# Split buffers for rounded and low weight halves, a longer lead, and another order of the products in each weight tile

## The chip, the cores and the metric

The kernel runs on one core of a Trainium2 chip. The core has a matrix engine (TensorE, PE in the profile; PEld is its loading of the operand that stays in the array), a vector engine (VectorE, DVE), a scalar engine (ScalarE, ACT), GpSimd (POOL) and SyncE (SP), which here only starts DMA transfers. Each engine works through its own queue of instructions in order; semaphores tie the queues together. The metric is the time of one execution in microseconds (us).

## What is computed

Two residual layers over 256 tokens of width 2048: a stick-breaking attention layer, then a layer whose attention chooses 64 keys for each query with an indexer. Each is followed by a multi-layer perceptron (MLP) with squared ReLU and 8192 hidden features. Cut to what matters here:

```python
for i in range(2):
    h = rms_norm(x, norm_mix[i])
    x = x + (stick_breaking_mixer if i % 2 == 0 else dsa_mixer)(h, ...)
    h = rms_norm(x, norm_mlp[i])
    x = x + jnp.square(jax.nn.relu(h @ w_up[i])) @ w_down[i]
```

All inputs are float32. The weights are about 390 MB and each is read once, so there is one pass over them.

## The kernel before

**Products in two halves.** TensorE multiplies in a rounded float32 format. To keep accuracy, each operand is split: `wh` is the weight tile rounded (ACT copies it into the rounded type, L946 through the helper at L101), `wl` is what the rounding left (DVE subtracts, L947). The activations are kept in the same two halves. Each product is then three matmuls: x high with `wh`, x high with `wl`, x low with `wh` (L217 to L219, and L376 to L378). Where the weights are the stationary operand (`feats_out`), the first and third are one matmul of 512 columns, since both halves of x stand side by side, and `wl` takes one of 256 (L239, L240).

**Tiles.** All weights are cut into tiles of 128 x 1024 (512 KB). The whole program is one list of items. An item has the raw tiles that it loads (`raws`), a `source` that gives the tile to split, a function `mm` that issues its matmuls, and a list `post` of functions to call after them. The main loop (from L968) takes the items in order: for item i it first splits item i + LEAD (LEAD = 2, L979), issues loads as buffers come free (L980), issues the item's matmuls (L981) and then what is in `post`. `wh` and `wl` lie in one tile `w` with three buffers. Raw tiles come in over SP's queue into `wraw` (five buffers) or `sraw` (four).

The order written is not quite the order on the engines: the program is built with a scheduler that draws up each engine's queue with the help of a timeline of its own (L1007). Only the first 16 items, where `pinned` holds, and the instructions marked one by one keep the order as written. Once drawn up, a queue is fixed.

**The MLP in blocks.** The up projection of a block of 1024 features is a product of 2 x 2 blocks, and for seven of the eight blocks in each MLP it is done with seven block products instead of eight (`seven`, L361). This needs sums of weight blocks, made on DVE: for each of four steps s, b11 + b12 (L402), then b12 + b22 on top of that (L403), then t = (b11 + b12) + b22 (L404), all three in `sums`, which is the source of the second of the four items in `first`; later t + b21 (L408), the source of the third of three items in `second`. `first` has 16 items, `second` 12, of six matmuls each. The four `first` items of a step use: b11 itself, b22 (after the sums), the first sum, the second sum.

Between these items stand tiles of the down projection of the block before (`down`, 12 matmuls an item): nine among `first`, then two, then five among `second` (SPAN, L49). So a period has 28 + 16 items. Block products gather in PSUM, in a pair of banks (`pair`) and in single banks `v`, `z`, `y`. `between` and `between2` (L430, L435) combine those after `first`; `after` and `after2` (L439, L445) after `second`, on DVE into `se`. Then ACT applies ReLU and square (`square_up`, L338). `turn` (L449) transposes the finished block on PE (L455), eight transposes into an accumulator, and ACT and DVE split it into the halves of the next down projection's operand (L457 through L101, and L458). `ends` (L460) lists these steps by their distance in items from the end of `second`: 0, 1, 2, 3, 5 and 7 items on, among the items of the next block. The down projection's results are added to the residual on DVE (`add_residual`, L261).

There are three accumulators of two banks each (`accp`): a pair of block products, the running down projection, and the turns share them. Two single banks (`auxp`) serve the rest.

Of the kernel before, what the change touches and what calls it, by code (L numbers as in the profile page):

```python
# [16 lines left out]
P = 128  # L17
D = 2048
S = 256
# [24 lines left out]
RAW = 5  # L44
LEAD = 2
PINNED = 16
# [3 lines left out]
EARLY = 5  # L50
RAWS = {"wraw": RAW, "sraw": 4}
BANK = 128
# [10 lines left out]
class Item:  # L63


    def __init__(self, raws, a, b, mm, moving=False, source=None):
        self.raws, self.a, self.b, self.mm, self.moving, self.post = raws, a, b, mm, moving, []
        self.source = source or (lambda: raws[0].ap)

# [6 lines left out]
def trunk(ctx, tc, x, norm_mix, w_in_a, w_out_a, w_in_b, w_out_b, q_norm_b, k_norm_b, rel_bias,  # L76
# [126 lines left out]
    def tokens_out(items, key, w, r0, c0, lhs, q, done, n=KT, apart=False):  # L203


        def mm(wh, wl):
            if q == 0 and apart:
                accs[key] = [auxp.tile([P, 512], F32, name="aux") for _ in range(2)]
            elif q == 0:
                acc = accp.tile([P, 2, 512], F32, name="acc")  # L210
                accs[key] = [acc[:, t, :] for t in range(2)]
            acc = accs[key]
            for t in range(2):
                for j in range(KB):
                    k = KB * q + j
                    ts = slice(t * P, (t + 1) * P)
                    pin(pe.matmul(acc[t], lhs(k, 0, ts), wh[:, j, :], start=(k == 0), stop=False))  # L217
                    pin(pe.matmul(acc[t], lhs(k, 0, ts), wl[:, j, :], start=False, stop=False))  # L218
                    pin(pe.matmul(acc[t], lhs(k, 1, ts), wh[:, j, :], start=False,  # L219
                                  stop=(k == n - 1)))  # L220
# [8 lines left out]
    def feats_out(items, key, w, c0, q, done):  # L229

        def mm(wh, wl):
            if q == 0:
                accs[key] = accp.tile([P, 2, 512], F32, name="acc")
            acc = accs[key]
            for j in range(KA):
                k = KA * q + j
                for m in range(2):
                    ms = slice(m * P, (m + 1) * P)
                    pe.matmul(acc[:, m, :], wh[:, j, ms], xT[:, k, :, :], start=(k == 0), stop=False)  # L239
                    pe.matmul(acc[:, m, 0:S], wl[:, j, ms], xT[:, k, 0, :], start=False,  # L240
                              stop=(k == KT - 1))
        it = plain(rows(w, KA * P * q, KA * P, c0, 256), KA, 256, mm)
# [3 lines left out]

    def joined(acc):

        c = tmp.tile([P, 2, S], F32, name="jc")
        u = tmp.tile([P, 2, S], F32, name="ju")  # L250
        copy(c, acc[:, :, S:])
        dve.tensor_add(u, acc[:, :, :S], c)
        return u
# [24 lines left out]
    def mlp(l, next_col):  # L278
# [63 lines left out]
        def up_done(h, s, acc):  # L342
            u = joined(acc)
            square_up(u)
# [16 lines left out]
        def seven(f, c0):  # L361
# [8 lines left out]
            def item(raws, bank, x, s, source, opens=True):  # L370
                def mm(wh, wl):
                    acc = bank()
                    on = dict(skip_group_check=not opens)
                    for j in range(KB):
                        k = KB * s + j
                        pe.matmul(acc, x(k, 0), wh[:, j, :], start=opens and k == 0, stop=False, **on)  # L376
                        pe.matmul(acc, x(k, 0), wl[:, j, :], start=False, stop=False, **on)  # L377
                        pe.matmul(acc, x(k, 1), wh[:, j, :], start=False, stop=k == HK - 1, **on)  # L378
                return Item(raws, KB, 512, mm, True, source)

# [15 lines left out]
            for s in range(HK // KB):  # L396
                b11, b12 = block(0, 0, s, "wraw"), block(0, 1, s, "sraw")
                b21, b22 = block(1, 0, s, "sraw"), block(1, 1, s, "sraw")

                def sums(s=s, b11=b11, b12=b12, b22=b22):  # L400
                    t = g["t", s] = temp().rearrange("p (a b) -> p a b", a=KB)
                    dve.tensor_add(b11.ap, b11.ap, b12.ap)  # L402
                    dve.tensor_add(b12.ap, b12.ap, b22.ap)  # L403
                    dve.tensor_add(t, b11.ap, b22.ap)  # L404
                    return b22.ap

                def last_sum(s=s, b21=b21):
# [41 lines left out]
            def turn(n, c0, c1):  # L449
# [3 lines left out]
                for k in range(4):  # L453
# [58 lines left out]
        for f in range(1, LASTF + 1):  # L512
            first, second, mid, ends = seven(f, 1024 * f)
            items += spread(first, ds[:n1])
            for n, e in late:
                items[n].post.append(e)
            at = len(items) - 1
            items += ds[n1:n1 + n2] + spread(second, ds[n1 + n2:n1 + n2 + n3])
            put(items, at, mid)
            at = len(items) - 1  # L520
            late = [(at + n, e) for n, e in enumerate(ends) if e]
            if f == LASTF:
                late = [(at + max(n - 1, 0), e) for n, e in enumerate(e for e in ends if e)]
            ds = ds[n1 + n2 + n3:]
        items += ds
        for n, e in late:
            items[n].post.append(e)
        return items, begin


    def mixer_a():
# [17 lines left out]
        def qk_done(which, hp, acc):  # L549
            u = joined(acc)  # L550
            r = mk([P, 2, S], which + "T")
# [113 lines left out]
    def mixer_b():  # L665
# [42 lines left out]
        def ki_done():  # L708
            acc = accs.pop("ki")
            c = tmp.tile([P, 2, S], F32, name="jc")[:, 0, :]  # L710
            u = tmp.tile([P, 2, S], F32, name="ju")[:, 0, :]
            copy(c[:80, :], acc[:80, 0, S:])
# [224 lines left out]

    def split(i):
        if i < len(items):
            it = items[i]  # L940
            pair = wpool.tile([P, 2 * WT + BANK], F32R, name="w")
            at = SHIFT if it.moving else 0
            wh, wl = (pair[:, at + h * WT:at + h * WT + it.a * it.b].rearrange(
                "p (a b) -> p a b", a=it.a) for h in range(2))
            raw = it.source()
            copy(wh, raw)  # L946
            pin(dve.tensor_sub(wl, raw, wh.bitcast(F32)))  # L947
            parts[i] = wh, wl

    for n in range(4):  # L950
# [60 lines left out]
```

## Time and profile before

| What | Value |
|---|---|
| median of 3 runs | 2174.95 us (2173.22 to 2175.07) |
| the profiled execution's own time | 2174.56 us |
| its span, first to last instruction | 2172.8 us |
| mean granted clock of TensorE | 0.991 |
| read from memory | 391.82 MB, 183 GB/s over the span |
| a 512 KB weight load, issue to landing | 3.5 to 4.6 us (median by tensor) |

The span of one profiled execution is a little shorter than its time, because the time has the start and the end of the execution as well. A row of the timeline reads: start, duration, engine, line, operation, output and input tile, shapes, count; in brackets the engine's idle time before it and what ended it. A row of the list of waits reads: who, for whom, then total us, times, and longest us. Matmuls overlap in the records: a matmul of 512 columns is shown with 0.39 us, though the next begins 0.23 us later, so lengths are taken from start to start. L101 is a helper's line: many of ACT's copies carry it, and the tile's name tells them apart.

### The profile page before, as it was taken

The page shows a single profiled execution, that of the slowest core. Times are in us where ns is not written, and L with a number is a line of the kernel's source. Part 1 is how long each engine was busy: PE and PEld are TensorE (multiplying, and loading weights), DVE is VectorE, ACT ScalarE, POOL GpSimd, SP SyncE. Part 2 cuts the span into 40 slices and gives each one's busy share as a digit, 9 for nine tenths or more (in the row PEclk, how much of TensorE's full clock was granted, in tenths as well). Part 3 has the DMA queues.
Part 4 walks back from the last instruction along what each step waited for, and adds up shares of the span by engine and source line. Part 5 has one row for each costly group of instructions (what it writes and reads, how often), then busy time and mean ns, then how long its engine had stood idle before and what let it go on. Part 6 is the DMA issues. An engine that isn't in the chain of part 4 may idle for free.

```text
span 2172.8 us, 26216 instructions
## 1 busy us (share of the span) xinstructions
PE 2107.2 (97%) x9764; PEld 1720.2 (79%) x9764; DVE 1719.7 (79%) x1833; ACT 1256.8 (58%) x1560; POOL 28.2 (1%) x71
## 2 busy tenths in 40 slices
PE   8999999999999999999999999999999999999999
PEld 7888888877777777777888788887777777777787
DVE  5466665898898888988865877689989898888985
ACT  5455555666566565655654556566656556565563
POOL 0100010000000000000000000000000000000000
PEclk9999999999999999999999999999999999999999
DMA  7667655665555646555466564466555555555544
GB/s 235 191 190 192 177 169 179 200 222 165 191 186 165 222 140 210 176 182 198 140 205 185 158 189 160 151 218 207 171 194 175 186 192 174 196 172 184 180 155 160
DMA packets 241396, 398.85 MB, mean 184 GB/s; under 512 B 14578, under 2 KB 80756, under 8 KB 241268
## 3 DMA queue, kind: packets, MB, share of 16 engines
q1 hardware_dynamic: 233508, 389.74, 55.8%
q10 hardware_dynamic: 7760, 7.43, 1.2%
q8 instruction: 76, 1.25, 0.3%
q14 instruction: 52, 0.43, 0.1%
HBM read 391.82 MB, written 5.23 MB: 183 GB/s over the span
## 4 chain that ended last, share of the span: by engine, by line
PE 70%; DVE 20%; issue 5%; ACT 3%; DMA 2%; DVEq 0%; ACTq 0%
PE acc L218 14%; PE acc L219 14%; PE acc L217 13%; DVE w L947 9%; PE acc L239 7%; PE acc L240 4%; PE acc L377 3%; PE acc L376 3%; PE acc L378 3%; DVE wraw L402 2%; DVE t L404 2%; ACT w L101 2%; DVE sraw L403 2%; DVE xs L261 2%; PE aux L377 2%
## 5 line engine op out<-in xcount | busy, mean ns | idle before, releaser
L947 DVE TENSOR_TENSOR w<-wraw,w 128x1024 fp32r<-128x1024 f32 x626 | 758.1, 1222 | 317.3 <-ACT w L101 312.8
L101 ACT ACTIVATE w<-wraw 128x1024 fp32r<-128x1024 f32 x626 | 664.6, 1062 | 587.3 <-PE acc L219 443.1
L218 PE MATMUL acc<-w,hS 128*128 128x512 f32 x1008 | 402.4, 399 | 10.0 <-DVE w L947 9.1
L217 PE MATMUL acc<-w,hS 128*128 128x512 f32 x1008 | 398.5, 396 | 0.1
L219 PE MATMUL acc<-w,hS 128*128 128x512 f32 x1008 | 398.0, 395 | 0.0
L239 PE MATMUL acc<-xT,w 128*128 128x512 f32 x896 | 314.2, 391 | 0.0
L101 ACT ACTIVATE w<-sraw 128x1024 fp32r<-128x1024 f32 x224 | 237.9, 1062 | 112.8 <-PE acc L219 60.8
L947 DVE TENSOR_TENSOR w<-sraw,w 128x1024 fp32r<-128x1024 f32 x224 | 273.4, 1221 | 27.8 <-ACT w L101 23.7
L240 PE MATMUL acc<-xT,w 128*128 128x256 f32 x896 | 253.4, 284 | 1.4 <-DVE w L947 1.2
L218 PEld LDWEIGHTS acc<-w,hS 128*128 128x128 f32 x1008 | 193.3, 192 | 59.4 <-DVE w L947 21.3
L217 PEld LDWEIGHTS acc<-w,hS 128*128 128x128 f32 x1008 | 192.1, 191 | 44.7 <-ACT w L101 4.0
L219 PEld LDWEIGHTS acc<-w,hS 128*128 128x128 f32 x1008 | 192.6, 191 | 39.8
L239 PEld LDWEIGHTS acc<-xT,w 128*128 128x128 f32 x896 | 168.1, 188 | 33.8
L240 PEld LDWEIGHTS acc<-xT,w 128*128 128x128 f32 x896 | 169.3, 189 | 3.9 <-DVE w L947 2.6
L217 PE MATMUL acc<-w,xT 128*128 128x512 f32 x320 | 127.8, 399 | 2.5 <-ACT w L101 2.5
L218 PE MATMUL acc<-w,xT 128*128 128x512 f32 x320 | 126.5, 395 | 0.5 <-DVE w L947 0.5
L219 PE MATMUL acc<-w,xT 128*128 128x512 f32 x320 | 126.4, 395 | 0.0
L376 PE MATMUL acc<-w,xS 128*128 128x512 f32 x224 | 94.8, 423 | 9.1 <-ACT w L101 9.1
L218 PE MATMUL acc<-w,oT 128*128 128x512 f32 x256 | 101.7, 397 | 0.0
L217 PE MATMUL acc<-w,oT 128*128 128x512 f32 x256 | 101.0, 395 | 0.0
L219 PE MATMUL acc<-w,oT 128*128 128x512 f32 x256 | 100.3, 392 | 0.0
L261 DVE SCALAR_TENSOR_TENSOR xs<-acc,rs,xs 128x512 f32<-128x512 f32 x120 | 84.3, 744 | 18.0 <-PE acc L219 18.0
(207 smaller groups left out, 3033.4 us busy)
## 6 DMA issues: line engine op xcount, KB each, us to landing
wraw<-in_w_down_dram SPq DMA_DIRECT2D x256, 512.0 KB, 4.6
sraw<-in_w_up_dram SPq DMA_DIRECT2D x168, 512.0 KB, 4.5
wraw<-in_w_in_a_dram SPq DMA_DIRECT2D x96, 512.0 KB, 4.0
wraw<-in_w_up_dram SPq DMA_DIRECT2D x88, 512.0 KB, 4.5
wraw<-in_w_in_b_dram SPq DMA_DIRECT2D x64, 512.0 KB, 3.7
wraw<-in_w_out_a_dram SPq DMA_DIRECT2D x32, 512.0 KB, 3.5
wraw<-in_w_out_b_dram SPq DMA_DIRECT2D x32, 512.0 KB, 3.8
bv_d<-bv ACTq DMA_DIRECT2D x4, 766.0 KB, 8.8
```

The source lines that it names most:

```text
L101: pin(act.activation(o, i, AF.Copy, scale=scale))
L217: pin(pe.matmul(acc[t], lhs(k, 0, ts), wh[:, j, :], start=(k == 0), stop=False))
L218: pin(pe.matmul(acc[t], lhs(k, 0, ts), wl[:, j, :], start=False, stop=False))
L219: pin(pe.matmul(acc[t], lhs(k, 1, ts), wh[:, j, :], start=False, stop=(k == n - 1)))
L239: pe.matmul(acc[:, m, :], wh[:, j, ms], xT[:, k, :, :], start=(k == 0), stop=False)
L240: pe.matmul(acc[:, m, 0:S], wl[:, j, ms], xT[:, k, 0, :], start=False, stop=(k == KT - 1))
L261: dve.scalar_tensor_tensor(xc, acc[t], scale[:, t:t + 1], xc, op0=OP.mult, op1=OP.add)
L376: pe.matmul(acc, x(k, 0), wh[:, j, :], start=opens and k == 0, stop=False, **on)
L377: pe.matmul(acc, x(k, 0), wl[:, j, :], start=False, stop=False, **on)
L378: pe.matmul(acc, x(k, 1), wh[:, j, :], start=False, stop=k == HK - 1, **on)
L402: dve.tensor_add(b11.ap, b11.ap, b12.ap)
L947: pin(dve.tensor_sub(wl, raw, wh.bitcast(F32)))
```

## The change

1. `wh` and `wl` get tiles of their own, with LEAD + 2 = 5 and LEAD + 1 = 4 buffers; LEAD is 3. In the main loop the low half of item i + 3 is made, then loads are issued, then the rounded half of item i + 4.
2. Each item's matmuls with `wh` come first, those with `wl` after them.
3. The three sums are no longer one step. The second item of a step has b22 itself as its source, the third item's source makes the first sum, the fourth's the second; the third sum comes after the fourth item's low half (`then`). `b11`, `b12` and `b22` are held until there. `sraw` has five buffers.
4. `ends` are placed by the us of the items' matmuls (2.72 an item, half of it for block items) instead of by their number: 0, 1.4, 1.4, 2.8, 8.0 and 10.8 us. The second step of the sums after `second` thereby comes one item later, the second turn one item earlier; in the last block, where whole items follow, the second step moves one item later.
5. Room: the tile `ju` of `joined` moves from a pool shared by all sections into the sections (in the MLP it takes a `t2` buffer), and the scratch for dynamic DMA is cut to 1024. `between2` is attached to the same item as before.
6. At the start three items are split before the first matmul, with the rounded half of a fourth, and the second half of the first 512 columns of x is transposed before the first item's matmuls instead of behind them.

```diff
-LEAD = 2
+LEAD = 3
+TURNS = (8.0, 10.8)
-RAWS = {"wraw": RAW, "sraw": 4}
+RAWS = {"wraw": RAW, "sraw": 5}
...
-            for t in range(2):
-                for j in range(KB):
-                    k = KB * q + j
-                    ts = slice(t * P, (t + 1) * P)
-                    pin(pe.matmul(acc[t], lhs(k, 0, ts), wh[:, j, :], start=(k == 0), stop=False))
-                    pin(pe.matmul(acc[t], lhs(k, 0, ts), wl[:, j, :], start=False, stop=False))
-                    pin(pe.matmul(acc[t], lhs(k, 1, ts), wh[:, j, :], start=False,
-                                  stop=(k == n - 1)))
+            for w, parts in ((wh, (0, 1)), (wl, (0,))):
+                for t in range(2):
+                    for j in range(KB):
+                        k = KB * q + j
+                        for part in parts:
+                            pin(pe.matmul(acc[t], lhs(k, part, slice(t * P, (t + 1) * P)), w[:, j, :],
+                                          start=w is wh and part == 0 and k == 0,
+                                          stop=w is wl and k == n - 1))
...
-                def sums(s=s, b11=b11, b12=b12, b22=b22):
-                    t = g["t", s] = temp().rearrange("p (a b) -> p a b", a=KB)
-                    dve.tensor_add(b11.ap, b11.ap, b12.ap)
-                    dve.tensor_add(b12.ap, b12.ap, b22.ap)
-                    dve.tensor_add(t, b11.ap, b22.ap)
-                    return b22.ap
+                def two(b11=b11, b12=b12):
+                    dve.tensor_add(b11.ap, b11.ap, b12.ap)
+                    return b11.ap
+
+                def other(b12=b12, b22=b22):
+                    dve.tensor_add(b12.ap, b12.ap, b22.ap)
+                    return b12.ap
+
+                def three(s=s, b11=b11, b22=b22):
+                    t = g["t", s] = temp().rearrange("p (a b) -> p a b", a=KB)
+                    dve.tensor_add(t, b11.ap, b22.ap)
...
                 first += [item([b11], pair(0), quarter(0, 0), s, lambda b=b11: b.ap),
-                          item([b12, b22], single("v"), summed(3), s, sums),
-                          item([], single("z"), summed(0), s, lambda b=b11: b.ap),
-                          item([], pair(1), summed(2), s, lambda b=b12: b.ap)]
-                first[-2].uses = [b11]
-                first[-1].uses = [b12]
+                          item([b22], single("v"), summed(3), s, lambda b=b22: b.ap),
+                          item([b12], single("z"), summed(0), s, two),
+                          item([], pair(1), summed(2), s, other)]
+                first[-1].then, first[-1].uses = three, [b11, b12, b22]
...
-            ends = [after, after2,
-                    lambda: (square_up(se(2)), square_up(se(1))),
-                    lambda: (square_up(se(0)), square_up(g["s2"])),
-                    None, lambda: turn(1, se(2), se(1)), None, lambda: turn(0, se(0), g["s2"])]
+            ends = [(0, after), (1.4, after2), (1.4, lambda: (square_up(se(2)), square_up(se(1)))),
+                    (2.8, lambda: (square_up(se(0)), square_up(g["s2"]))),
+                    (TURNS[0], lambda: turn(1, se(2), se(1))), (TURNS[1], lambda: turn(0, se(0), g["s2"]))]
...
-    def split(i):
+    def half(it, name, bufs):
+        home = wpool.tile([P, WT + BANK], F32R, name=name, bufs=bufs)
+        at = SHIFT if it.moving else 0
+        return home[:, at:at + it.a * it.b].rearrange("p (a b) -> p a b", a=it.a)
+
+    def high(i):
         if i < len(items):
             it = items[i]
-            pair = wpool.tile([P, 2 * WT + BANK], F32R, name="w")
-            at = SHIFT if it.moving else 0
-            wh, wl = (pair[:, at + h * WT:at + h * WT + it.a * it.b].rearrange(
-                "p (a b) -> p a b", a=it.a) for h in range(2))
-            raw = it.source()
+            wh, raw = half(it, "wh", LEAD + 2), it.source()
             copy(wh, raw)
+            parts[i] = wh, raw
+
+    def low(i):
+        if i < len(items):
+            it = items[i]
+            wh, raw = parts[i]
+            wl = half(it, "wl", LEAD + 1)
             pin(dve.tensor_sub(wl, raw, wh.bitcast(F32)))
             parts[i] = wh, wl
+            if it.then:
+                it.then()
...
-        split(i)
+        high(i)
+        low(i)
         loads(i, 1)
-    items[0].post.append(lambda: prep(0, 0, False, (1,)))
+        if i == 1:
+            prep(0, 0, False, (1,))
+    high(LEAD)
...
-        split(i + LEAD)
+        low(i + LEAD)
         loads(i + LEAD)
+        high(i + LEAD + 1)
         it.mm(*parts.pop(i))
```

More of the change, by code (lines that the diff above doesn't have):

```diff
@@ L67, in __init__ @@
         self.raws, self.a, self.b, self.mm, self.moving, self.post = raws, a, b, mm, moving, []
-        self.source = source or (lambda: raws[0].ap)
+        self.source, self.then, self.us = source or (lambda: raws[0].ap), None, 2.72
 def plain(src, a, b, mm, moving=False):
@@ L234, in mm @@
             acc = accs[key]
[L235 to L241, printed above, removed]
+            for w, cs, xs_ in ((wh, slice(0, 2 * S), slice(0, 2)), (wl, slice(0, S), 0)):
+                for j in range(KA):
+                    k = KA * q + j
+                    for m in range(2):
+                        pe.matmul(acc[:, m, cs], w[:, j, m * P:(m + 1) * P], xT[:, k, xs_, :],
+                                  start=w is wh and k == 0, stop=w is wl and k == KT - 1)
         it = plain(rows(w, KA * P * q, KA * P, c0, 256), KA, 256, mm)
@@ L245, in feats_out, with joined @@
         items.append(it)
-    def joined(acc):
+    def joined(acc, u):
         c = tmp.tile([P, 2, S], F32, name="jc")
-        u = tmp.tile([P, 2, S], F32, name="ju")
         copy(c, acc[:, :, S:])
@@ L342, in up_done @@
         def up_done(h, s, acc):
-            u = joined(acc)
+            u = joined(acc, temp()[:, :2 * S].rearrange("p (a b) -> p a b", a=2))
             square_up(u)
@@ L373, in mm @@
                     on = dict(skip_group_check=not opens)
[L374 to L379, printed above, removed]
+                    for w, parts in ((wh, (0, 1)), (wl, (0,))):
+                        for j in range(KB):
+                            k = KB * s + j
+                            for part in parts:
+                                pe.matmul(acc, x(k, part), w[:, j, :],
+                                          start=opens and w is wh and part == 0 and k == 0,
+                                          stop=w is wl and k == HK - 1, **on)
+                it = Item(raws, KB, 512, mm, True, source)
+                it.us /= 2
+                return it
             def pair(n):
@@ L514, in mlp @@
             items += spread(first, ds[:n1])
[L515 to L523, printed above, removed]
+            put(items, len(items) - 1, mid[:1])
+            items += ds[n1:n1 + n2]
+            put(items, len(items) - n2, mid[1:])
+            items += spread(second, ds[n1 + n2:n1 + n2 + n3])
+            late.append((len(items) - 1, ends))
             ds = ds[n1 + n2 + n3:]
         items += ds
-        for n, e in late:
-            items[n].post.append(e)
+        for n, ends in late:
+            at = 0
+            for us, f in ends:
+                while at < us:
+                    n, at = n + 1, at + items[n + 1].us
+                items[n].post.append(f)
         return items, begin
@@ L549, in qk_done @@
         def qk_done(which, hp, acc):
-            u = joined(acc)
+            u = joined(acc, mk([P, 2, S], "ju"))
             r = mk([P, 2, S], which + "T")
@@ L710, in ki_done @@
             c = tmp.tile([P, 2, S], F32, name="jc")[:, 0, :]
-            u = tmp.tile([P, 2, S], F32, name="ju")[:, 0, :]
+            u = mk([P, S], "ju")
             copy(c[:80, :], acc[:80, 0, S:])
@@ L995 @@
     from concourse.bass_utils import run_bass_kernel_spmd
-    nc = bacc.Bacc("TRN2", target_bir_lowering=False, num_devices=1)
+    nc = bacc.Bacc("TRN2", target_bir_lowering=False, num_devices=1,
+                   dynamic_dma_scratch_size=1024)
     arrays, args = {}, []
```

## The prediction

> **What bounds the kernel now.** I read the busy shares first, then what the TensorE waits for, then each stretch of the multi-layer perceptron (MLP) by itself.
>
> ```profile
> PE 2107.2 (97%) x9764; PEld 1720.2 (79%) x9764; DVE 1719.7 (79%) x1833; ACT 1256.8 (58%) x1560; POOL 28.2 (1%) x71
> ```
>
> The TensorE (PE) is busy 97% of the span. So a change that adds and removes no matmul can only win two things: PE's gaps, and matmuls that run slower than they could. The shares also average stages with different limits. The windows by stage show where the loss lies. Columns: window, its length, then busy time and (instructions) of PE, PEld, DVE, ACT and POOL, then granted clock, DMA share, GB/s.
>
> ```profile
> core 0 of [0], span 2172.8 us
> core 0: us, PE busy (x) PEld busy (x) DVE busy (x) ACT busy (x) POOL busy (x), PEclk, DMA share, GB/s
> 425.00:521.00 96.00, 92.50 (x422) 74.52 (x420) 87.63 (x86) 62.05 (x70) 0.00 (x0) 1.00 0.56 183
> 521.41:981.71 460.30, 439.56 (x1881) 349.38 (x1881) 405.94 (x381) 272.70 (x286) 0.00 (x0) 0.98 0.56 183
> 705.45:797.38 91.93, 87.79 (x377) 69.90 (x377) 81.19 (x77) 54.54 (x58) 0.00 (x0) 0.98 0.57 183
> 1425.00:1564.00 139.00, 135.31 (x655) 111.47 (x653) 124.35 (x140) 91.10 (x117) 0.00 (x0) 1.00 0.60 195
> 1564.14:1654.73 90.59, 86.41 (x377) 68.70 (x377) 81.20 (x77) 54.51 (x58) 0.00 (x0) 1.00 0.55 186
> 1654.73:2022.65 367.92, 351.31 (x1505) 279.67 (x1505) 324.78 (x305) 218.23 (x229) 0.00 (x0) 0.98 0.56 183
> ```
>
> The seven-product blocks repeat: ten periods take 460.30 + 90.59 + 367.92 = 918.81 us, **91.9 us each**. A period holds 16 down tiles of 12 matmuls, 28 block tiles of 6 (360 in all, 512 columns each) and 16 transposes. What PE needs for them I take from start-to-start steps, since the shown durations overlap:
>
> ```profile
> 604.79 0.39 PE L378 MATMUL acc<-w,xT 128*128 128x512 f32 x1
> ...
> 605.47 0.39 PE L378 MATMUL acc<-w,xT 128*128 128x512 f32 x1
> 529.64 0.27 PE L455 MATMUL acc<-ident,se 128*128 128x128 f32 x1
> ...
> 530.40 0.27 PE L455 MATMUL acc<-ident,jc 128*128 128x128 f32 x1
> ```
>
> Three steps in 0.68 us give 0.227 us a matmul; seven steps in 0.76 us give 0.109 us a transpose. So 360 x 0.227 + 16 x 0.109 = **83.4 us**. PE loses 8.5 us of each period, although DVE needs only 81.2 and idles 10.7. Neither engine is full: each waits for the other, because the weight halves are made only two tiles ahead (three `w` buffers). The losses have two places. The first is a run of sums:
>
> ```profile
> 899.13 1.22 DVE L947 TENSOR_TENSOR w<-sraw,w 128x1024 fp32r<-128x1024 f32 x1
> 900.27 1.22 DVE L402 TENSOR_TENSOR wraw<-wraw,sraw 128x1024 f32<-128x1024 f32 x1
> 901.41 1.21 DVE L458 TENSOR_TENSOR hS<-acc,hS 128x1024 fp32r<-128x1024 f32 x1
> 902.54 1.21 DVE L403 TENSOR_TENSOR sraw<-sraw 128x1024 f32<-128x1024 f32 x1
> 903.67 1.22 DVE L404 TENSOR_TENSOR t<-wraw,sraw 128x1024 f32<-128x1024 f32 x1
> 904.81 2.35 DVE L947 TENSOR_TENSOR w<-wraw,w 128x1024 fp32r<-128x1024 f32 x2
> ```
>
> From 899.13 to 904.81 DVE (one instruction after another, 1.135 us apart) makes no low half: three sums and L458 stand in between. PE's own rows show the price:
>
> ```profile
> 904.17 0.50 PE L376 MATMUL aux<-w,xS 128*128 128x512 f32 x1
> 905.30 0.50 PE L376 MATMUL acc<-w,xS 128*128 128x512 f32 x1 [0.62 <-ACT w L101]
> 906.08 0.50 PE L218 MATMUL acc<-w,hS 128*128 128x512 f32 x1 [0.28 <-DVE w L947]
> ```
>
> 904.17 to 906.08 is 1.91 us for two matmuls, 1.46 us lost, the second a tile whose low half is late. The second place is the turn, where PE transposes the finished block:
>
> ```profile
> 513.43 0.39 PE L378 MATMUL acc<-w,xT 128*128 128x512 f32 x1
> ...
> 517.23 0.68 DVE L443 TENSOR_TENSOR se<-se,acc 128x512 f32<-128x512 f32 x1
> ...
> 521.41 0.33 PE L455 MATMUL acc<-ident,se 128*128 128x128 f32 x1 [1.58 <-ACT se L340]
> ```
>
> The last block product issues at 513.43, but L443, its first user on DVE, begins only at 517.23, behind low halves and a sum; ACT's squares then end late and PE waits 1.58 us. The list of waits counts it:
>
> ```profile
> PE acc L455 <- ACT se L340: 21.2, 24, 1.6
> ```
>
> 24 waits, two a turn: twelve turns, so **twelve such periods**, 12 x 8.5 = 102 us in all. The wait also costs clock (stretches as above, the granted clock last but two):
>
> ```profile
> 518.74:522.15 3.41, 1.64 (x8) 0.83 (x7) 3.41 (x4) 3.41 (x7) 0.00 (x0) 1.00 0.00 0
> 522.15:525.57 3.42, 3.42 (x13) 2.94 (x12) 3.42 (x4) 2.21 (x3) 0.00 (x0) 0.50 0.86 260
> 1564.05:1567.46 3.41, 3.13 (x16) 2.45 (x17) 3.41 (x5) 2.94 (x5) 0.00 (x0) 1.00 0.60 190
> ```
>
> After a 3.41 us stretch with PE busy 1.64 the next runs at half clock: 1.7 us lost by 3.42 x 0.5. The period that begins at 1564.14 keeps its clock and is 1.3 us shorter than that of 705.45. I take 1.5.
>
> A period's 8.5 us thus hold: turn wait 1.8 (2.0 with the uneven steps), cold clock 1.5, sum and low-half waits about 3 (two places like the one shown), and 2 of slow steps after waits.
>
> **The change, part by part.** No arithmetic goes or comes: 45 or so subtractions and 16 sums a period stay, so PE's floor stays 83.4 and DVE's 81.2.
>
> *Buffers and lead.* Low halves three tiles ahead instead of two, high halves four. A block tile is 6 x 0.227 = 1.36 us of PE, a down tile 2.72; the mix in the first stretch (16 and 9) averages 1.85. One tile more is 1.85 us in which DVE may be late.
>
> *Rounded products first.* Before, the low half is wanted at the second matmul of a tile. Now 8 of 12 (4 of 6) matmuls go first: another 1.8 us on a down tile, 0.9 on a block tile. Together with the lead, DVE may be about 3 us later than now. The same matmuls run in another order; in the 256-row form (L239/L240) the 256-column ones now stand in a row. The trace has such a pair:
>
> ```profile
> 296.34 0.28 PE L591 MATMUL acc<-sph,tri 128*128 128x256 f32 x1
> 296.46 0.28 PE L592 MATMUL acc<-spl,tri 128*128 128x256 f32 x1
> ```
>
> 0.12 us a step, under the 0.227 of 512 columns, about in proportion: nothing gained or lost. I cost the order at zero there.
>
> *Does 3 us do?* In a first stretch PE needs 16 x 1.36 + 9 x 2.72 + 1.7 = 48.0 us. DVE needs 25 low halves and 12 sums at 1.135 (42.0), four half-size additions, two L458 and three pairs of residual updates (about 2.4 + 2.3 + 4.0): 50.7. It falls behind by 2.7, and by about 3.6 in the first quarter, where the turn's work stands. The rest of the period gives it back: PE 7 x 2.72 + 12 x 1.36 = 35.4 against DVE about 28.6. The slack at the start is three tiles and two thirds of the fourth, less one low half: 3.67 x 1.85 - 1.1 = 5.7 us. It covers 3.6. With two tiles and no more it was 2 x 1.85 - 1.1 = 2.6, and did not.
>
> *Sums singly.* At most one sum before a low half instead of three: the 1.46 us shown should go. But the source of the first, second and last sum is now copied right after it (add, then ACT's copy, then the subtraction); `v` no longer waits for sums at all. The new chain is rival two.
>
> *Turns.* Both are placed by time: after 8.0 us of PE work the first (the same tile as before, the fifth on), after 10.8 the second (the sixth, before the seventh). The second difference step moves one tile on. Before, PE came to the turn early because its order had been drawn up round late halves; with fewer late halves it should come later, and DVE reach L443 sooner. But the two turns share what is left of three accumulators, so the second waits for ACT's copy and L458 of the first, about 1.0 + 1.2 us against one down tile of 2.72: hidden, up to 1 us if DVE is behind.
>
> *Loads.* Same number, sizes and queue (SP). A fifth `sraw` buffer comes; but the b11 block in `wraw` is now held until the third sum, one or two tiles longer. The slot's next user is some seven tiles later, over 10 us of PE work, so I cost this at zero; if it shows, it is rival four. *The two ends.* One more tile is prepared ahead and four transposes come before tile 0: cold, 4 x 0.22 = 0.9 us at most, against tile 0 no longer stopping at its second matmul; zero, between -1 and +1. At the end token half 0 is ready two matmuls before the end instead of six: up to 0.9 later; I take 0.5.
>
> *The sum.* Left of 8.5 in a period: turn 0.6, cold 0.3, late halves 0.8, slow steps 0.5: 2.2. So 6.3 x 12 = 76 less. The stretches before the first turn of each MLP idle 3.5 + 3.7 us; 70% of it goes, 5. With the end: 76 + 5 - 0.5 = 80. The profiled execution took 2174.56 us (its span of 2172.8 and 1.8 around it), 0.4 below the median of 2174.95. **2174.56 - 80 = 2094 us**; bounds 2072 (1 us left in a period less) to 2112.
>
> **Rivals.** *One: the floor.* All waits go and DVE idles no more than 2 us a period: 102 + 7 saved, about 2066; 10 lower if slow steps in the stretches outside go too. For it: slack 5.7 against 3.6. Against: DVE at 81.2 of 83.4 leaves no room for any wait of its own.
>
> *Two, half open: DVE becomes the bound.* Twelve sums a period (first, second, last) are followed by ACT's copy, then DVE's subtraction:
>
> ```profile
> L101 ACT ACTIVATE w<-wraw 128x1024 fp32r<-128x1024 f32 x626 | 664.6, 1062 | 587.3 <-PE acc L219 443.1
> 590.02 1.22 DVE L408 TENSOR_TENSOR sraw<-t,sraw 128x1024 f32<-128x1024 f32 x1
> 591.16 1.40 DVE L261 SCALAR_TENSOR_TENSOR xs<-acc,rs,xs 128x512 f32<-128x512 f32 x2
> 592.48 1.21 DVE L947 TENSOR_TENSOR w<-t,w 128x1024 fp32r<-128x1024 f32 x1
> ```
>
> If nothing else stands in DVE's queue between, it idles about 1.1 us (the copy's 1062 ns), and all low halves behind wait. Today's only such chain, L408, is filled: other work follows the sum. With half of the twelve open DVE needs 81.2 + 6.6 = 87.8: 4.1 x 12 = 49 saved, 2125 to 2130.
>
> *Two, all open: slower.* 81.2 + 12 x 1.1 = 94.4, or 2.5 over today's 91.9; with a further 0.5 of waits that it triggers, 3.0 x 14 blocks = 42 more: **2217**. It decides from (91.9 - 81.2) / 1.1 = 10 of the twelve.
>
> *Three: the cold clock stays although the wait goes.* If the transposes and not the gap cool the array, 1.2 x 12 = 14 is not saved: 2108. Against: the 1564.14 period has the same 377 PE instructions at clock 1.00. The Trainium skill, "TensorE: Matmul & The Clock Gate", Part 4, says that transposes don't count as PE-busy for the clock gate; by it this rival would hold, and the sum would be 2108. The same page asks in its closing table for no PE gap over about 3 us; here a gap of 1.58 us was followed by half clock, so the trace disagrees with that limit.
>
> *Four: raw tiles are short, not halves.* The stretch 518.74 has 0 GB/s: all raw buffers were held. If so, the lead can't be used; only the sums' spread counts, (3 - 0.8) x 12 = 26 saved, 2148 (to 2175 where the longer hold eats it). For: b11 is held longer. Against: DVE was behind there, which holds raw tiles by itself.
>
> **How the numbers follow.** Forecast 0.44; floor 0.14; half open 0.14; all open 0.10; cold stays 0.10; raw tiles 0.08. The range 2056 to 2148 takes the forecast, most of the floor, half open, cold stays, and a third of the raw tiles: 0.8. About 0.2% (4 us) is what a measurement of this kernel can tell from no change. Faster 0.88, within it 0.02 (from raw tiles), slower 0.10.
>
> **What would show it.** Right: periods near 85.6 us, DVE busy still 81 of them, the wait for L340 gone from the list or under 7 us, clock 1.00 in most windows, no run of three sums. Wrong: DVE idle before the subtractions that follow the sums L402, L403 and L408 (rival two); half clock without a wait before it (three); ACT waiting for DMA (four). A period still over 90 us would make the whole argument wrong.

## The result, and the profile after

The changed kernel takes **2070.84 us** (median of 4 runs, 2070.56 to 2071.21) against 2175.01 us before (median of 4): the ratio is 0.9522, 95% interval 0.9505 to 0.9538. That is 104 us less, where 80 were forecast; it lies in the range, 23 us under the predicted 2094.

The page of the profile after, the busy share of each engine:

```profile
PE 2057.0 (99%) x9764; PEld 1712.0 (83%) x9764; DVE 1702.1 (82%) x1833; ACT 1212.8 (59%) x1560; POOL 34.0 (2%) x71
```

The same numbers of instructions on every compute engine in a shorter time: no work went, only waiting and slow steps. The windows by stage (columns as before), a period of the seven-product blocks and the two stretches ahead of the first turn of each MLP:

```profile
core 0: us, PE busy (x) PEld busy (x) DVE busy (x) ACT busy (x) POOL busy (x), PEclk, DMA share, GB/s
604.75:688.34 83.59, 83.59 (x378) 69.08 (x377) 80.06 (x77) 50.97 (x59) 0.00 (x0) 1.00 0.62 201
425.00:521.00 96.00, 95.36 (x449) 79.46 (x449) 91.52 (x92) 64.70 (x77) 0.00 (x0) 1.00 0.59 191
1425.00:1512.00 87.00, 86.36 (x400) 71.70 (x399) 82.52 (x80) 57.80 (x68) 0.00 (x0) 1.00 0.64 204
```

A period now lasts 83.59 us, from first transpose to first transpose of the turn, against 91.9 before and the worked-out floor of 83.4. PE has no gap in it, the granted clock (the share of its full clock that TensorE was given) is 1.00, and DVE is busy 80.06 us, 96% of it. 91.9 - 83.6 = 8.3 us in each of twelve periods is 100 of the 104 us. What is left of PE's waits, in the list of waits of the whole run (who, for whom, total us, times, longest):

```profile
PE aux L136 <- DMA graw<-in_norm_mix_dram: 4.2, 1, 4.2
PE aux L377 <- ACT wh L102: 1.3, 2, 0.6
PE aux L861 <- DVE pl L850: 1.3, 1, 1.3
PE aux L158 <- DMA xs<-in_x_dram: 0.9, 1, 0.9
PE acc L219 <- ACT wh L102: 0.5, 1, 0.5
```

In the kernel before, the same list had, behind the wait for L340 (21.2 us), these rows for late halves:

```profile
PE acc L218 <- DVE w L947: 9.5, 24, 0.5
PE acc L376 <- ACT w L101: 9.1, 14, 0.9
PE aux L376 <- ACT w L101: 8.9, 12, 0.7
```

The wait for L340 is gone, and of the waits for halves 1.8 us are left (L377 and L219 above). The one thing that looks different from the source's plan is DVE's order in a first stretch (timeline of DVE):

```profile
718.99 1.22 DVE L404 TENSOR_TENSOR wraw<-wraw,sraw 128x1024 f32<-128x1024 f32 x1
720.24 1.22 DVE L408 TENSOR_TENSOR sraw<-sraw 128x1024 f32<-128x1024 f32 x1
721.38 1.22 DVE L413 TENSOR_TENSOR t<-wraw,sraw 128x1024 f32<-128x1024 f32 x1
722.52 2.35 DVE L961 TENSOR_TENSOR wl<-wraw,wh 128x1024 fp32r<-128x1024 f32 x2
```

The three sums, which the source makes singly, stand in a row again: the scheduler put them there. And PE does not stop for them. There are 56 such steps (four in each of 14 blocks). In DVE's order in the trace, 26 of them have no low half between the first and the third sum; before it was 52. So what carried the gain had to be tried part by part.

### The profile page after: what moved, and what is told of

Read it like the earlier page. It is cut to its first block, busy times and chain, and to the rows that moved or that the text cites. A ratio compares the mean times of both kernels' runs of the same rounds, so it can differ in the third digit from the quotient of the medians.

```text
span 2069.5 us, 26597 instructions
## 1 busy us (share of the span) xinstructions
PE 2057.0 (99%) x9764; PEld 1712.0 (83%) x9764; DVE 1702.1 (82%) x1833; ACT 1212.8 (59%) x1560; POOL 34.0 (2%) x71
## 4 chain that ended last, share of the span: by engine, by line
PE 99%; DVE 0%; ACT 0%; DMA 0%; issue 0%; DVEq 0%; ACTq 0%
PE acc L219 52%; PE acc L240 15%; PE acc L377 15%; PE aux L377 11%; PE acc L462 1%; PE aux L158 1%; PE aux L830 1%; PE aux L219 1%; PE aux L610 0%; PE acc L566 0%; PE acc L744 0%; PE aux L847 0%; PE aux L808 0%; PE acc L709 0%; DMA xs<-in_x_dram 0%; PE aux L611 0%
## 5 line engine op out<-in xcount | busy, mean ns | idle before, releaser
L961 DVE TENSOR_TENSOR wl<-wraw,wh 128x1024 fp32r<-128x1024 f32 x626 | 755.5, 1220 | 222.7 <-PE acc L219 111.0
L102 ACT ACTIVATE wh<-wraw 128x1024 fp32r<-128x1024 f32 x626 | 647.0, 1054 | 459.8 <-PE acc L219 160.2
L219 PE MATMUL acc<-wh,hS 128*128 128x512 f32 x2016 | 503.7, 390 | 0.0
L219 PEld LDWEIGHTS acc<-wh,hS 128*128 128x128 f32 x2016 | 376.9, 188 | 80.0 <-ACT wh L102 2.3
L102 ACT ACTIVATE wh<-sraw 128x1024 fp32r<-128x1024 f32 x224 | 233.5, 1054 | 184.3 <-DVE sraw L416 127.7
L961 DVE TENSOR_TENSOR wl<-sraw,wh 128x1024 fp32r<-128x1024 f32 x224 | 271.1, 1221 | 40.4 <-PE acc L377 23.0
L219 PE MATMUL acc<-wl,hS 128*128 128x512 f32 x1008 | 270.3, 389 | 0.0
L240 PE MATMUL acc<-xT,wh 128*128 128x512 f32 x896 | 230.4, 396 | 0.0
L219 PEld LDWEIGHTS acc<-wl,hS 128*128 128x128 f32 x1008 | 189.2, 188 | 39.1
L219 PE MATMUL acc<-wh,xT 128*128 128x512 f32 x640 | 165.5, 398 | 0.5 <-ACT wh L102 0.5
L219 PEld LDWEIGHTS acc<-wh,xT 128*128 128x128 f32 x640 | 120.0, 190 | 27.6 <-issue 2.3
L219 PE MATMUL acc<-wh,oT 128*128 128x512 f32 x512 | 133.1, 395 | 0.0
L377 PE MATMUL aux<-wh,xS 128*128 128x512 f32 x448 | 123.1, 395 | 1.3 <-ACT wh L102 1.3
L377 PE MATMUL acc<-wh,xS 128*128 128x512 f32 x448 | 124.0, 392 | 0.0
L377 PE MATMUL acc<-wh,xT 128*128 128x512 f32 x448 | 120.1, 389 | 0.0
L219 PEld LDWEIGHTS acc<-wh,oT 128*128 128x128 f32 x512 | 94.7, 188 | 18.8
L377 PEld LDWEIGHTS aux<-wh,xS 128*128 128x128 f32 x448 | 82.1, 188 | 21.0 <-ACT wh L102 5.3
L377 PEld LDWEIGHTS acc<-wh,xT 128*128 128x128 f32 x448 | 84.0, 188 | 17.4
L377 PEld LDWEIGHTS acc<-wh,xS 128*128 128x128 f32 x448 | 83.1, 188 | 16.8
```

Of the source, the lines that this page charges most:

```text
L102: pin(act.activation(o, i, AF.Copy, scale=scale))
L219: pin(pe.matmul(acc[t], lhs(k, part, slice(t * P, (t + 1) * P)), w[:, j, :], start=w is wh and part == 0 and k == 0, stop=w is wl and k == ...
L240: pe.matmul(acc[:, m, cs], w[:, j, m * P:(m + 1) * P], xT[:, k, xs_, :], start=w is wh and k == 0, stop=w is wl and k == KT - 1)
L377: pe.matmul(acc, x(k, part), w[:, j, :], start=opens and w is wh and part == 0 and k == 0, stop=w is wl and k == HK - 1, **on)
```

## The experiments

Four theories were set against each other. *Slack*: what counts is how late DVE may be with a low half, from whichever part. *Order*: that the low half is wanted late. *Sums*: that three sums in a row are the loss. And, for the other sign, *rival two*: that a sum followed by ACT's copy and the subtraction idles DVE unless other work fills the place.

**One part alone, put into the kernel before.**

The lead:

```diff
-LEAD = 2
+LEAD = 3
...
-            pair = wpool.tile([P, 2 * WT + BANK], F32R, name="w")
+            pair = wpool.tile([P, 2 * WT + BANK], F32R, name="w", bufs=LEAD + 1)
```

(The smaller DMA scratch makes the room, here and in the run of the sums.)

> The kernel before with the lead alone: LEAD 3, four buffers of the joint tile w (and the smaller DMA scratch for room); products in the old order, sums in one step. Slack theory: DVE may be 3 x 1.85 - 1.1 = 4.4 us late instead of 2.6, against a backlog of about 3.6, so most of the 8.5 us a period goes: 2080 to 2100 us. Order theory (the low half wanted late is what counts): little changes, 2150 to 2175. Sums theory (runs of three sums are the loss): the sums still stand together, 2130 to 2160.

Measured: 2081.9 us, ratio to before 0.9577 (0.9562 to 0.9591): 92 us less, most of the gain, from a longer lead with one more buffer of the old kind. The windows of two periods:

```profile
534.17:618.65 84.48, 84.21 (x377) 68.88 (x378) 80.25 (x77) 53.55 (x58) 0.00 (x0) 1.00 0.63 200
618.65:703.17 84.52, 84.25 (x377) 68.89 (x378) 80.23 (x77) 53.49 (x58) 0.00 (x0) 1.00 0.61 199
```

84.5 us, within 1.1 of the floor, clock 1.00: the turn's wait went without the turn being moved in the source. One thing more changed, though the source leaves it alone: in the trace a low half now stands between the sums in 54 of the 56 steps (before: 4). The scheduler moved it there.

The order of products (the changed `mm` loops of `tokens_out`, `feats_out` and `item`, nothing else):

```diff
-            for t in range(2):
-                for j in range(KB):
...
+            for w, parts in ((wh, (0, 1)), (wl, (0,))):
+                for t in range(2):
```

> The kernel before with the order of products alone: rounded products first, lead 2, three joint buffers, sums in one step. Slack theory: slack 2.6 + 0.9 to 1.8 = 3.5 to 4.4 us, just about the backlog of 3.6: 2085 to 2120 us. Order theory: nearly all goes, 2075 to 2085. If the lead alone counts: 2160 to 2175.

Measured: 2116.4 us, ratio 0.9735 (0.972 to 0.9749): 58 us less. The time lies at the slow end of what the slack theory expected. Here too the scheduler broke up the sums, in all 56 steps (timeline of DVE, L403 to L405 are the three sums):

```profile
630.11 1.22 DVE L403 TENSOR_TENSOR wraw<-wraw,sraw 128x1024 f32<-128x1024 f32 x1
631.25 1.22 DVE L948 TENSOR_TENSOR w<-sraw,w 128x1024 fp32r<-128x1024 f32 x1
632.38 1.22 DVE L404 TENSOR_TENSOR sraw<-sraw 128x1024 f32<-128x1024 f32 x1
633.52 1.22 DVE L405 TENSOR_TENSOR t<-wraw,sraw 128x1024 f32<-128x1024 f32 x1
```

So the 58 us belong to the order of products together with the queue that the scheduler drew up for it; how much each brings was not separated. Broken-up sums are not the whole gain of the lead: this kernel has them in every step and is 34 us slower than the lead alone.

The sums (`two`, `other`, `three`, `then`, and the fifth `sraw` buffer):

```diff
-                          item([b12, b22], single("v"), summed(3), s, sums),
+                          item([b22], single("v"), summed(3), s, lambda b=b22: b.ap),
+                          item([b12], single("z"), summed(0), s, two),
...
-RAWS = {"wraw": RAW, "sraw": 4}
+RAWS = {"wraw": RAW, "sraw": 5}
```

> The kernel before with the sums made singly (b22 as the second item's source, third sum after the fourth item's low half, sraw with five buffers), lead 2 and the old order of products. Sums theory: the late halves go, about 3 us a period, 2135 to 2145 us. Slack theory: the backlog is as long as before and the slack 2.6, so it stays within 20 us of before, 2155 to 2180; the new chain sum, copy, subtraction may make it slower.

Measured: 2175.69 us, ratio 1.0005 (0.9995 to 1.0014): nothing. Its list of PE's waits could be that of before:

```profile
PE acc L459 <- ACT se L340: 21.3, 24, 1.6
PE acc L218 <- DVE w L951: 9.7, 25, 0.5
PE aux L376 <- ACT w L101: 9.0, 12, 0.7
PE acc L376 <- ACT w L101: 8.8, 14, 0.6
```

The timeline of DVE shows why; L401, L405 and L410 are the three sums:

```profile
729.22 1.22 DVE L401 TENSOR_TENSOR wraw<-wraw,sraw 128x1024 f32<-128x1024 f32 x1
730.47 1.23 DVE L405 TENSOR_TENSOR sraw<-sraw 128x1024 f32<-128x1024 f32 x1
731.62 1.22 DVE L410 TENSOR_TENSOR t<-wraw,sraw 128x1024 f32<-128x1024 f32 x1
```

They stand where they stood before. All 9764 instructions of PE, 1833 of DVE and 1560 of ACT have the same order in the two traces: the new source gave the same queues. So this run says nothing about the sums theory. What speaks against it is the kernel after: PE has no gap in its period although 26 of the 56 steps have no low half between the sums. Whether runs of sums cost anything at lead 2 is not shown by any run.

The turns, two items later:

```diff
-                    None, lambda: turn(1, se(2), se(1)), None, lambda: turn(0, se(0), g["s2"])]
+                    None, None, None, lambda: turn(1, se(2), se(1)), None, lambda: turn(0, se(0), g["s2"])]
```

> The kernel before with both turns two items later (seventh and ninth item after the block instead of fifth and seventh), nothing else. Gap theory (PE's wait before the turn cools the clock): if the wait goes, the half-clock windows go too, 12 x (2.0 + 1.5) = 42 us less, 2130 to 2140, granted clock 1.00. If the transposes themselves cool the clock: wait gone but clock still 0.991, 2148 to 2155. If DVE's backlog only moves the wait elsewhere: 2160 to 2180.

Measured: 2175.02 us, ratio 1.0000 (0.9991 to 1.0009). The third expectation held: the wait moved. In its list of PE's waits L455 is no longer there, and a block tile's wait, 9.1 us before, has grown in its place; the timeline of PE shows one such wait:

```profile
PE acc L376 <- ACT w L101: 37.8, 14, 3.1
```

```profile
613.14 0.75 PE L376 MATMUL acc<-w,xS 128*128 128x512 f32 x1 [3.04 <-ACT w L101]
```

So the wait before the turn was not a loss of its own: once the turn was moved away, PE paid at the tile that it came to first. What was late there, ACT's timeline shows:

```profile
608.49 1.07 ACT L101 ACTIVATE w<-wraw 128x1024 fp32r<-128x1024 f32 x1 [0.34 <-PE acc L378]
609.45 1.13 ACT L339 ACTIVATE se<-se 128x512 f32<-128x512 f32 x2
610.49 0.61 ACT L339 ACTIVATE jc<-jc 128x512 f32<-128x512 f32 x1
611.01 1.13 ACT L340 ACTIVATE se<-se 128x512 f32<-128x512 f32 x2
612.05 1.04 ACT L101 ACTIVATE w<-sraw 128x1024 fp32r<-128x1024 f32 x1
```

The copy that PE waits for (612.05) stands behind five of the block's ReLU and square steps (L339 and L340), and these start right behind a copy that had itself waited for PE (608.49). So at this place the rounded half is late, in ACT's queue, and not a low half of DVE. The windows around that gap:

```profile
609.80:613.20 3.40, 0.35 (x2) 0.06 (x1) 3.40 (x4) 3.40 (x7) 0.00 (x0) 1.00 0.14 22
613.20:616.60 3.40, 3.40 (x8) 2.73 (x9) 1.86 (x2) 0.41 (x1) 0.00 (x0) 0.50 0.89 298
```

A gap and no transpose near it (the next one begins at 620.13), and the next 3.4 us run at half clock.

**One part undone, in the kernel after.**

```diff
-LEAD = 3
+LEAD = 2
```

> The kernel after with LEAD 2 (low halves two tiles ahead, rounded three; buffers four and three). Slack theory: slack 2.67 x 1.85 - 1.1 = 3.8 against a backlog of about 3.6, as with the order alone (2116), perhaps better for rounded halves made one tile earlier: 2095 to 2120 us. Order theory: 2071 to 2085.

Measured: 2103.24 us, ratio to before 0.9668 (0.9653 to 0.9682), 32 us slower than after. PE waits for rounded halves again:

```profile
PE acc L377 <- ACT wh L102: 13.2, 28, 1.6
```

The old order of products (the loops of before back in):

> The kernel after with the old order of products (x high with rounded, x high with low, x low with rounded). Slack theory: slack 4.4, as with the lead alone (2082): 2078 to 2090 us. If the order is what brings the last waits down: over 2090.

Measured: **2065.54 us**, ratio 0.9495 (0.948 to 0.9509): 5.3 us *faster* than the kernel after (no run above 2066.48, none of after below 2070.56). The slack theory had expected 2078 at best. So with the lead and the buffers in place the new order isn't only unneeded; it costs. Where, the windows of the first layer's attention show, 150 us each, of before, after and this kernel in this order:

```profile
150.00:300.00 150.00, 150.00 (x876) 133.51 (x875) 97.90 (x101) 80.90 (x94) 15.10 (x24) 1.00 0.62 180
```

```profile
150.00:300.00 150.00, 150.00 (x868) 131.54 (x867) 96.47 (x101) 80.19 (x92) 19.61 (x22) 1.00 0.62 176
```

```profile
150.00:300.00 150.00, 150.00 (x875) 133.40 (x874) 97.23 (x100) 79.89 (x94) 18.63 (x23) 1.00 0.63 179
```

PE is busy throughout in all three, but takes 876, 868 and 875 matmuls in the same time. The share of each kind in the window isn't quite equal, so 0.8% is only about right; but the kernel with the old order keeps pace with before, and the new order doesn't. From the 600th to the 1500th of PE's instructions it is 154.5 us before, 156.0 after and 154.6 here: 1.4 of the 5.3 us. The rest is spread thinly and isn't assigned.

The sums in one step again:

> The kernel after with the three sums in one step again, as the source of the second item (sraw keeps five buffers). Since the scheduler sets sums in runs of three even in the kernel after, both theories that don't count the sums expect 2070 to 2078 us. Sums theory: 2090 to 2110.

Measured: 2068.33 us, ratio 0.9508 (0.9492 to 0.9524), 2.5 us faster than after, which is less than the 4 us that the prediction took for the least that can be told. The two queues of DVE differ little (1823 of 1833 instructions are in the same order), so again the source's sums were hardly tried.

**The other sign.** Each sum and each low half of a block tile is tied behind the instruction written before it on DVE, so that the scheduler can't place them. This stops the fill, and every other shift of these instructions too:

```diff
-                    dve.tensor_add(b11.ap, b11.ap, b12.ap)
+                    tc.keep_in_program_order(dve.tensor_add(b11.ap, b11.ap, b12.ap))
...
-            pin(dve.tensor_sub(wl, raw, wh.bitcast(F32)))
+            sub = dve.tensor_sub(wl, raw, wh.bitcast(F32))
+            if pinned[0] or it.us < 2:
+                tc.keep_in_program_order(sub)
```

(and the same at the other three sums.)

> The kernel after, but in the seven-product blocks each sum and each low half of a block tile is tied behind the instruction written before it on DVE, so that the scheduler can't put other work between a sum and the subtraction that waits for ACT's copy of it. Rival two: twelve chains a period stand open, each idles DVE about 1.1 us, 81.2 + 13 = 94.4 us a period against 83.6 now: 2190 to 2215 us, DVE idle before L961 on ACT. If filling doesn't matter: 2071 to 2080.

Measured: 2192.71 us, ratio to before 1.0085 (1.0068 to 1.0102): 122 us slower than after and slower than before, with every buffer and the longer lead in place. A row of DVE's list of waits, here and then in the kernel after, one open chain in its timeline, and a period's window:

```profile
DVE wl L961 <- ACT wh L102: 123.4, 124, 2.9
```

```profile
DVE wl L961 <- ACT wh L102: 23.0, 26, 1.4
```

```profile
701.54 1.22 DVE L416 TENSOR_TENSOR sraw<-t,sraw 128x1024 f32<-128x1024 f32 x1
702.68 0.68 DVE L449 TENSOR_TENSOR se<-aux,se 128x512 f32<-128x512 f32 x1
703.97 1.23 DVE L961 TENSOR_TENSOR wl<-sraw,wh 128x1024 fp32r<-128x1024 f32 x1 [0.61 <-ACT wh L102]
```

```profile
553.10:645.30 92.20, 87.64 (x378) 70.20 (x377) 80.45 (x78) 50.58 (x57) 0.00 (x0) 0.96 0.56 183
```

Here a half-size addition fills 0.6 us of ACT's copy, and DVE still idles the rest. It idles 92.2 - 80.45 = 11.8 us a period. That alone would say little, since it idled 10.7 before; but it now waits for ACT's copies 100 us longer than in the kernel after. Rival two is a real mechanism; the scheduler's order is what keeps it nearly shut.

**What the lead alone lacks, and the clock once more.** Between the lead alone (2081.9) and the kernel after with the old order (2065.5) lie 16 us. `a_os` is the kernel after with the old order and the sums in one step; the next two change one thing in it:

> The kernel after with the old order of products and the three sums in one step: buffers, lead and turns alone stay. If the small gains of the two (5.3 and 2.5 us) add up: 2062 to 2065 us. If both came from the same place (the first stretches and the start): 2065 to 2067.

Measured: 2066.1 us, ratio 0.9501 (0.9487 to 0.9516). The two small gains don't add up.

```diff
-            ends = [(0, after), (1.4, after2), (1.4, lambda: (square_up(se(2)), square_up(se(1)))),
+            ends = [(0, after), (0.7, after2), (2.7, lambda: (square_up(se(2)), square_up(se(1)))),
...
-TURNS = (8.0, 10.8)
+TURNS = (8.0, 12.2)
```

> The same as a_os, with the steps after a block at the items of the kernel before (second difference one item earlier, second turn one item later). If the turns' places are what the lead alone (2082) lacks: 2070 to 2082 us, with waits at the turn. If separate buffers and the rounded half a fourth tile ahead are: within 3 us of a_os.

Measured: 2066.12 us, ratio 0.9502 (0.9486 to 0.9518). But the trace has 208 of the 224 transposes at the same place in PE's queue as `a_os`; only those of the last block of each MLP moved. The scheduler had set the turns itself. So the source's new places aren't needed, and what other places in the queue would cost this run doesn't say.

```diff
-        low(i + LEAD)
+        high(i + LEAD)
+        low(i + LEAD)
         loads(i + LEAD)
-        high(i + LEAD + 1)
```

> The same as a_os, but the rounded half is made three tiles ahead like the low half, not four (the buffers stay five and four). If the fourth tile is what the lead alone (2082) lacks: 2072 to 2085 us, PE or DVE waiting for ACT's copies. If not: within 3 us of a_os.

Measured: 2065.61 us, ratio 0.9499 (0.9485 to 0.9513). Here too the queues are nearly those of `a_os`: all but two of PE's 9764 instructions, all but one of DVE's 1833 and 1522 of ACT's 1560 are in the same order. So the fourth tile was hardly taken away, and its worth is open. Of the 16 us between 2081.9 and 2066, about 12 lie in the twelve periods: a window of one in `a_os` has 83.51 us, against 84.5 with the lead alone. Whether the split into two buffers, the fifth `sraw` buffer, the queue that comes of them or another part brings it was not separated.

Last, the turns of the kernel after put early:

```diff
-TURNS = (8.0, 10.8)
+TURNS = (2.8, 5.4)
```

> The kernel after with the turns put early, 2.8 and 5.4 us of matmuls after a block instead of 8.0 and 10.8, so that PE may have to wait for ACT's squares although DVE is not behind. Gap theory: if PE waits 1.5 us or more there, the clock falls to half for a stretch of 3.4 us and the period grows by the wait and up to 1.7 us: 2090 to 2125 us, clock 0.98 to 0.995. If the scheduler fills the place with other matmuls: 2068 to 2080, clock 1.00.

Measured: 2088.32 us, ratio 0.9604 (0.959 to 0.9618), 17.5 us slower than after. That is neither expectation: PE waits fourteen times, once a block, and yet the clock stays (its list of PE's waits, and a window around one of them):

```profile
PE aux L377 <- ACT wh L102: 17.5, 14, 1.6
```

```profile
610.00:613.40 3.40, 2.13 (x16) 1.60 (x14) 3.40 (x4) 2.99 (x3) 0.00 (x0) 1.00 0.44 124
```

The waits fall on a tile's rounded half, not on the transposes, and the sum of them (17.5) is as large as the loss. ACT's timeline shows the reason:

```profile
610.28 1.94 ACT L102 ACTIVATE hS<-acc 128x1024 fp32r<-128x1024 f32 x2 [2.65 <-PE acc L462]
612.21 1.06 ACT L102 ACTIVATE wh<-wraw 128x1024 fp32r<-128x1024 f32 x1
```

The copy that PE needs at 613.32 stands in ACT's queue behind the copies of both turns, and before those ACT idles 2.65 us for PE's transposes. Here a turn that comes too early does cost what PE waits.

## Why the prediction was right, and where it was not

*The bound and the stage: right.* PE's gaps and slow steps in twelve periods carried the loss, and the floor of 83.4 us a period, worked out from step lengths, came out as 83.59.

*What makes up for it: right in kind, but not proven alone.* Lead and order each bring much by themselves, as slack would. Beside the estimate of how late DVE may be stand the steps, of 56, with a low half between the sums in the trace, and the time:

| Kernel | estimated slack, us | sums broken up | time, us |
|---|---|---|---|
| before | 2.6 | 4 | 2175 |
| before, new order | 3.5 to 4.4 | 56 | 2116 |
| after, lead 2 | 3.8 | 54 | 2103 |
| before, lead 3 | 4.4 | 54 | 2082 |
| after, old order | 4.4 | 42 | 2066 |
| after | 5.7 | 30 | 2071 |

From before to 4.4 us, the more slack, the less is lost. It isn't a law: the two rows with 4.4 differ by 16 us, the row with 5.7 is not the fastest, and the row with 3.8 lies above the estimated backlog of 3.6 and is still 32 us slower than after. No run shows the backlog itself, and all rows with lead 2 but the first have their sums broken up as well. With lead 3 and the new order sums in a row cost PE nothing; how much they cost at lead 2 stays open.

*"Left of 8.5 in a period: turn 0.6, cold 0.3, late halves 0.8, slow steps 0.5: 2.2": mis-sized.* Measured is 83.59 - 83.4 = 0.2. The difference of 2.0 us, times twelve, is 24 us, as much as the whole distance between 2094 and 2071. I kept 2.2 because DVE at 81.2 of 83.4 seemed to leave no room; the run shows that it needs 80.06 and PE still never waits. The first rival, the floor at 2066, was nearly the case that came about (DVE idles 83.59 - 80.06 = 3.5 us a period where it said 2), and 0.14 was too little for it: my own slack of 5.7 against 3.6 spoke for it.

*The turn and the cold clock as terms of their own: wrong in kind.* `b_turns` moved the turns; the 21.2 us of waits went, those for L376 rose from 9.1 to 37.8, and the time stayed. Both were the price of weight halves made too late; in `b_lead`, with a longer lead, both went together. That DVE's late L443 held the turn was read too simply: L443 ended at 517.91 (517.23 + 0.68), but ACT began the squares at 519.18, straight behind a copy of a rounded half that had waited for PE (ACT's timeline before):

```profile
518.21 1.07 ACT L101 ACTIVATE w<-wraw 128x1024 fp32r<-128x1024 f32 x1 [0.34 <-PE acc L378]
519.18 1.14 ACT L339 ACTIVATE se<-se 128x512 f32<-128x512 f32 x2
```

As in `b_turns`, the wait runs through ACT's queue.

*"The 1.46 us shown should go" through single sums: wrong.* `b_sums` changed no queue, and in the kernel after the three stand in a row all the same in 22 of 56 steps. The rows of PE beside it were read too simply: of the 1.46 us, 0.62 is PE's wait for ACT's copy and only 0.28 that for a low half. That those waits went all the same came with the longer lead, not with this part. The step that failed is that source order was taken for queue order, though the prediction had said that the scheduler draws up the queue.

*The order of products at zero in the step length: wrong by up to 5 us,* against the pair of 256-column steps that I had quoted; which of the matmul's forms pays was not separated. Its gain was real before (58 us, with the sums broken up along with it) and is nothing once the lead and the buffers stand.

*Rival two: right in mechanism, a little large in price.* 13.2 us of idle a period expected, 11.8 measured; 2217 expected for all chains open, 2193 measured. It did not come about in the kernel after since the scheduler fills most of the chains (23.0 us of such waits against 123.4), as the row of L408 had hinted.

*Rival three, cold clock through transposes: refuted for this kernel.* The kernel after has all its transposes, 377 or 378 PE instructions a period as before, at clock 1.00. The Trainium skill, "TensorE: Matmul & The Clock Gate", Part 4, says that transposes don't count as PE-busy; `b_turns` shows half clock after a gap without any transpose, and the kernel after shows transposes without half clock. If the rule holds, eight transposes in a row (0.9 us) are too few to matter here. *Rival four, raw tiles:* PE's list has no wait for a weight load; the two DMA waits are of the start. ACT waits for raw tiles 6.8 us in the whole run, against 1.3 before, and PE doesn't stop for it.

*The stretches before the first turn:* 5 us expected; PE's idle time in them fell from 3.5 + 3.7 to 0.64 + 0.64, about 5.9.

## What to carry to other kernels

Where two engines are both nearly full and each waits for the other, count how late the feeding engine gets within a period (its work minus the consumer's, cumulated) and compare it with the buffers' depth in us, as an estimate that ranks kernels rather than times them; one more buffer may be worth more than any reordering. Waits at different lines may be one backlog paid at different places: move one wait alone, and see whether the time moves, before pricing it. Then look in the queue of each engine for what the late instruction stands behind: here it was ACT's, before the turn as well as in `b_turns` and `a_turns`. And where a scheduler draws up the queues, a change in the source is to be looked for in the engines' timelines before anything is put down to it: a run that leaves the queues as they were tries nothing, and one that changes a single line may change another part's order as well.

## What was not expected of the hardware

The granted clock fell after gaps shorter than a 3.4 us stretch, and not always. Before, a stretch with PE busy 1.64 of 3.41 us was followed by half clock; in the kernel with early turns one with 2.13 of 3.40 was not, nor did any of its fourteen waits (1.6 us at most) cool the clock. How the gap falls against the stretches matters. In the trace of before the half-clock stretches begin at 522.15, 614.31, 706.47 us and so on, each a whole multiple of 3.413 us from the first, while the gaps come about every 91.9 us. The one turn whose gap (1.57 us, to 1564.14) kept the clock has a border of these stretches inside the gap:

```profile
610.90:614.31 3.41, 1.64 (x8) 0.86 (x7) 3.41 (x4) 3.41 (x7) 0.00 (x0) 1.00 0.00 0
1559.80:1563.21 3.41, 2.76 (x12) 1.86 (x10) 3.41 (x6) 3.06 (x5) 0.00 (x0) 1.00 0.01 4
1563.21:1566.63 3.42, 2.30 (x12) 1.74 (x13) 3.42 (x4) 3.42 (x6) 0.00 (x0) 1.00 0.36 102
```

A limit in PE's busy time can't be read from these runs: of the stretches that the clock changes of each trace mark out, one with 1.77 us was followed by half clock in `a_pin` (from 467.90), and one with 1.66 us in `a_order` (from 1339.79, with a gap of 1.75 us) was not.

The closing table of the Trainium skill's page "TensorE: Matmul & The Clock Gate" asks for no PE gap over about 3 us; the 1.58 us of before was enough in eleven turns of twelve.
